# Seven half products for three pairs of projection tiles, and rotary rows turned in groups

## The chip, the cores and the metric

The kernel runs on one core of a Trainium2 chip. The metric is the device time of one execution in microseconds, as the median of the runs shown; lower is better. Engines are named as in the profile: PE does the matmuls (PEld its weight loads), DVE the element-wise work on two operands, ACT copies and activations, POOL small moves and accumulating transfers, SP issues the other transfers.

## What is computed

One encoder layer for 512 tokens of 1024 features in float32: two attention mixers side by side, merged by gates, then a SwiGLU channel mixer. Cut to what matters here:

```python
proj = h @ w_in[l]
qa, ka, va, qb, kb, vb = jnp.split(proj, SPLITS, axis=-1)
qa = rope_partial(qa.reshape(b, s, A_Q_HEADS, HEAD_DIM), pos)      # 16 heads of 64
qb = rope_partial(...)  # and kb: 12 heads each, three groups of window and dilation
o_a = windowed_gqa_sink(qa, ka, va, a_sink[l])
o_b = dilated_mixture(qb, kb, vb)
gates = jax.nn.sigmoid(h @ w_gate[l] + b_gate[l])
g_a, g_b = jnp.split(gates, N_BRANCH, axis=-1)
mixed = g_a * (o_a @ w_br_a[l]) + g_b * (o_b @ w_br_b[l])
h = layer_norm(DN_ALPHA * h + mixed @ w_out[l], ln1_g[l], ln1_b[l])
f = (jax.nn.silu(h @ w_ff_gate[l]) * (h @ w_ff_up[l])) @ w_ff_down[l]
h = layer_norm(DN_ALPHA * h + f, ln2_g[l], ln2_b[l])
```
`rope_partial` turns only the first 16 of each head's 64 features by the token's position: 8 rows against 8 rows.

## The kernel before

**Products.** The projections are computed with features on the partitions and the 512 tokens on the columns. One weight unit is 1024 x 128: it gives one tile of 128 features (two heads) by 512 tokens. Each operand is split into a rounded upper part and a rest, and a product is three matmuls (upper x upper, upper x rest, rest x upper; lines 496 to 498 in `feat_k`). Over eight slices of 128 input features a unit is 24 matmuls of 512 columns. A unit's weights come in two halves (`half_unit`): SP loads a 128 x 512 half, ACT or DVE copies the upper part (`split`), DVE subtracts (line 383). The input is split in the same way at the start, into eight pairs that stay (lines 464 to 469).

**The channel mixer already uses seven half products.** Its two units of one index form a 2 x 2 block product over halves of the 1024 features and of the tokens (the `Quad` class): sums of weight blocks (S1 to S4) and of token blocks (T1 to T4) are formed and split, and seven products of 12 matmuls with 256 columns each take the place of eight (lines 1422 to 1424).

**Rotation.** A projected tile of queries or keys is turned by `rotate`: four DVE rows over all 128 partitions (lines 517 to 523), though only 16 of every 64 rows change. It is then split, and `q_post` and `k_post` move the parts to where the scores need them, by transfers from SP.

**Order.** Two things set it. `ORDER` is a list of steps written by hand: `VA` are the values of the first mixer, `q1` to `q7` and `k1` its query and key tiles (`q0`, `k0` come first of all), `A0` to `A3` its head groups of four heads and four blocks of queries each, `g` a gate tile, `Q00 K00` and so on the second mixer's query and key tiles, `V12 V0` its values, `B0` to `B3` its heads. Each step hands operations with their costs to a planner (`Program`). The planner goes through time with its own cost table and lets each engine take the first ready operation by priority, within limits on buffers: 85 slots of 128 x 512 in all, of them 6 for weights as loaded (`ws`), 12 for split weights (`whl`), the rest for general use, and eight PSUM banks, three of them for projections (`dense`). What it chose is the order in which each engine's instructions stand in the program; on the chip each engine works them off in that order and waits for what is not there yet.

**A head group** needs scores from PE, their minimum with mask and sink on DVE (line 798), the exponential on ACT (802), a reciprocal and a scaling (805, 739), transposes on PE (749), a split on ACT and DVE (754), the products with values on PE (815, 816), and a last sum on DVE (828). The values' own split is at 695.

**The end of the stage.** When the eight heads and groups are done, all slots go to the rest of the layer (`free_all`): branch products, gates times branches, output product, norm, channel mixer, norm.

Of the kernel before, what the change touches and what calls it, by code (L numbers as in the profile page):

```python
# [15 lines left out]
P = 128  # L16
# [44 lines left out]
UNITS = 2  # L61
SPIN = 4
# [6 lines left out]
N_WS, N_WHL, N_ATT = 6, 12, 16  # L69
# [10 lines left out]
g2 VA q1 A0 q2 q3 A1 g k1 q4 g q5 A2 g q6 g q7 A3 g2  # L80
Q00 K00 Q01 K01 V12 Q02 K02 V0 B0 Q10 K10 B1 Q11 K11 Q12 K12 B2 B3 g8
"""

# [34 lines left out]
class Program:  # L118
# [67 lines left out]
    def run(self):  # L186
# [26 lines left out]
        while n_left:  # L213
# [11 lines left out]
            while progress:  # L225
                progress = False
                for e in engines:
# [14 lines left out]
                    cost = dict(o.alts)[e]  # L242
# [12 lines left out]
                    if e == SP:  # L255
                        end = now + 0.47
                        moved = max(moved, now + 0.9) + (1.5 if now < 5 else 0.92) * cost
                        o.done = moved + 0.87
                    elif o.moves:
                        end = now + cost  # L260
                        moved = max(moved, end + 0.3) + 0.92 * o.moves
                        o.done = moved + (0.87 if e == ACT else 2.2)
                    else:
                        end = now + cost
                        o.done = end
# [50 lines left out]
def hybrid_layer(ctx: ExitStack, tc: tile.TileContext, wpack, xT, xtok, sink, bgate,  # L316
# [9 lines left out]
                  "ws": N_WS, "whl": N_WHL, "att": N_ATT, "gen": N_SLOT - 2 - N_ATT - N_WS - N_WHL,  # L326
# [34 lines left out]
    def f32(ap):  # L361
        return ap.bitcast(F32)

    def load(b, src, cost=0.73, prio=0.0, abs_prio=None, dst=None, after=()):
        return op([(SP, cost)], lambda e: nc.sync.dma_start(dst() if dst else b.t, src), writes=[b],
                  prio=prio, abs_prio=abs_prio, after=after)
# [21 lines left out]
    def half_unit(u, j):  # L388
        st, h, l = slot(F32, "ws"), slot(F32R, "whl"), slot(F32R, "whl")
        load(st, wpack[u, :, j * S:(j + 1) * S], prio=-LOOK)  # L390
        split(st, h, l, prio=-LOOK, hold=[(l, "room")])
        return h, l

# [61 lines left out]
    got = {}  # L455
    for j in range(KD):
        st, ap = slot(F32, "xs"), FIRST["x"][j]

# [51 lines left out]
    EV, NORM = -100.0, -150.0  # L510


    SHUF = list(range(8, 16)) + list(range(0, 8)) + list(range(16, 32))

    def rotate(ps):
        R, Sh = slot(), slot()
# [135 lines left out]
    def turned_values(u, nt, turn_by=0, done=None):  # L652
# [3 lines left out]
        for i in range(2):  # L656
# [16 lines left out]
            op(cp_alts(S, True, 0.3 if turn_by else 0.1)[:2 if turn_by else 1], evac, reads=[ps], writes=[t], prio=EV)  # L673
# [327 lines left out]

    def gate(f, put=False):
# [36 lines left out]
    env = {"gate": 0, "qs": {}, "ks": {}}  # L1039

    def step(w):
        if w == "VA":
# [15 lines left out]
        elif w[0] in "QK":  # L1058
            pair, g = int(w[1]), int(w[2])
            u = U_QKB + 6 * pair + 2 * g + (w[0] == "K")  # L1060
            if w[0] == "Q":
                env["qs"][pair, g] = dense_q(u, 4 if g == 0 else 0, (0, 1))
            else:
                env["ks"][pair, g] = dense_k(u, 8 if g == 0 else 0)
# [198 lines left out]
    def copy_by_act(dst, src, n, ps, reads, writes, prio=NORM):  # L1263
        op([(ACT, act(n, ps))], lambda e: copy(ACT, dst(), src()), reads=reads, writes=writes, prio=prio)

# [41 lines left out]
    LO, HI = slice(0, HP), slice(HP, S)  # L1307
    su, uf = {}, {}
    silus = []

    def tt(dst, x, y, o, reads, writes, w=HP, prio=EV):
        op([(DVE, dve(w))], lambda e: nc.vector.tensor_tensor(dst(), x(), y(), op=o), reads=reads, writes=writes,  # L1312
           prio=prio)

    def parts(h, l, src, reads, n, prio, whole=True):

        copy_by_act(h[0], src, n, False, reads, [h[1], l[2]], prio)
        tt(l[0], src, lambda: f32(h[0]()), ALU.subtract, [*reads, h[1]], [l[1]], n, prio)

    def hl(st, prio):  # L1320
        h, l = slot(F32R, "whl"), slot(F32R, "whl")
        parts((lambda: h.t, h), (lambda: l.t, l, (l, "room")), lambda: st.t, [st], S, prio)
        return h, l


# [451 lines left out]
```

## Time and profile before

| | us |
|---|---|
| median of 3 runs | 737.72 (737.66 to 737.75) |
| the profiled execution | 737.0 |
| its span, from the first to the last instruction | 735.2 |
| PE busy / DVE busy / ACT busy | 725.2 / 653.7 / 447.4 |

The span's times in windows and rows are microseconds from its start. A row in a timeline reads: start, busy time, engine, line, operation, what it writes and reads, partitions of the weights, shape and type, count; behind it in brackets the idle time before it and what ended that. Busy times of rows that follow each other overlap, so the distance of two starts is what a row costs on a full engine. A row in the list of waits reads: who waited, for whom, us in total, how often, the longest. The granted clock was 0.999 over the span.

### The profile page before, as it was taken

Reading aid. Unit: us, or ns where it says so; the run is one execution under the profiler, and the core shown is the slowest. Engines: PE = TensorE matmul, PEld = TensorE weight load, DVE = VectorE, ACT = ScalarE, POOL = GpSimd, SP = SyncE. Lnnn points to the kernel's source line nnn. Section 1 sums busy time; section 2 is a strip of 40 time slices with the busy share of each in tenths; the row PEclk is TensorE's granted clock in tenths of the full one; section 3 lists DMA queues with packets and bytes.
Section 4 is the critical chain, followed back from the end, with each engine's and each line's share of the span. In section 5 each row is a group of like instructions: output and inputs, shape, how many; then the busy total and the mean of one; then the engine's idle time right before and its main releaser. Section 6 shows DMA issues by size and latency. Waiting matters only on the chain.

```text
span 735.2 us, 13431 instructions
## 1 busy us (share of the span) xinstructions
PE 725.2 (99%) x4479; PEld 663.0 (90%) x4479; DVE 653.7 (89%) x1428; ACT 447.4 (61%) x1012; POOL 109.5 (15%) x273
## 2 busy tenths in 40 slices
PE   9999999999999999999999999999999999999995
PEld 6888888888888889888888999999999999999985
DVE  5879998898898999897686999799999999899977
ACT  5647687757665657774352567656666556666721
POOL 0000110000003323500010002111102111202100
PEclk9999999999999999999999999999999999999999
DMA  8824523437234765455583389776888978978402
GB/s 270 289 58 144 163 82 87 129 94 204 76 93 138 201 176 163 137 170 174 165 205 88 86 250 233 178 179 154 203 254 195 221 196 237 243 196 180 112 29 86
DMA packets 69252, 120.17 MB, mean 163 GB/s; under 512 B 8576, under 2 KB 12800, under 8 KB 69184
## 3 DMA queue, kind: packets, MB, share of 16 engines
q1 hardware_dynamic: 59040, 101.10, 44.7%
q0 software_dynamic: 9872, 18.09, 15.2%
q8 instruction: 35, 0.57, 0.3%
q14 instruction: 33, 0.27, 0.1%
q10 hardware_dynamic: 272, 0.13, 0.1%
HBM read 103.04 MB, written 2.10 MB: 143 GB/s over the span
## 4 chain that ended last, share of the span: by engine, by line
PE 94%; DMA 2%; DVE 2%; SPq 1%; ACT 1%; issue 0%; DVEq 0%; ACTq 0%
PE ps L497 12%; PE ps L496 12%; PE ps L498 12%; PE ps L1422 9%; PE ps L1424 9%; PE ps L1423 9%; PE ps L1633 4%; PE ps L1635 4%; PE ps L1634 4%; PE ps L749 3%; PE ps L1192 3%; PE ps L1193 3%; PE ps L1194 3%; PE ps L647 1%; PE ps L646 1%; PE ps L815 1%
## 5 line engine op out<-in xcount | busy, mean ns | idle before, releaser
L357 ACT ACTIVATE sl<-sl 128x512 fp32r<-128x512 f32 (+3 forms) x383 | 210.6, 582 | 62.0 <-DVE sl L1312 17.3
L1312 DVE TENSOR_TENSOR sl<-sl,sl 128x512 fp32r<-128x512 f32 (+3 forms) x294 | 167.1, 609 | 6.2 <-ACT sl L357 3.4
L357 ACT ACTIVATE sl<-ps 128x256 f32<-128x256 f32 (+5 forms) x205 | 85.8, 441 | 99.7 <-PE ps L1424 60.1
L496 PE MATMUL ps<-x,sl 128*128 128x512 f32 (+1 forms) x369 | 142.4, 386 | 0.3 <-ACT x L357 0.3
L498 PE MATMUL ps<-x,sl 128*128 128x512 f32 (+1 forms) x369 | 139.8, 379 | 0.0
L497 PE MATMUL ps<-x,sl 128*128 128x512 f32 (+1 forms) x337 | 127.9, 379 | 0.2 <-DVE x L469 0.2
L1422 PE MATMUL ps<-sl,sl 128*128 128x256 f32 x352 | 96.9, 275 | 0.6 <-ACT sl L357 0.6
L1423 PE MATMUL ps<-sl,sl 128*128 128x256 f32 x352 | 96.8, 275 | 0.0
L1424 PE MATMUL ps<-sl,sl 128*128 128x256 f32 x352 | 96.8, 275 | 0.0
L383 DVE TENSOR_TENSOR sl<-sl,sl 128x512 fp32r<-128x512 f32 x130 | 87.2, 685 | 5.1 <-ACT sl L357 4.5
L498 PEld LDWEIGHTS ps<-x,sl 128*128 128x128 f32 x369 | 69.9, 189 | 9.9 <-DVE sl L406 0.2
L496 PEld LDWEIGHTS ps<-x,sl 128*128 128x128 f32 x369 | 70.2, 190 | 8.7 <-ACT x L357 0.5
L371 POOL DMA_DIRECT2D sl<-wpack x44 | 38.5, 883 | 260.3 <-DMA sl<-wpack 72.7
L1422 PE MATMUL ps<-x,sl 128*128 128x256 f32 x264 | 72.6, 275 | 0.0
L1423 PE MATMUL ps<-x,sl 128*128 128x256 f32 x264 | 72.6, 275 | 0.0
L1424 PE MATMUL ps<-x,sl 128*128 128x256 f32 x264 | 72.6, 275 | 0.0
L497 PEld LDWEIGHTS ps<-x,sl 128*128 128x128 f32 x337 | 64.0, 190 | 7.5 <-DVE x L469 0.5
L1422 PEld LDWEIGHTS ps<-sl,sl 128*128 128x128 f32 x352 | 67.6, 192 | 0.8 <-ACT sl L357 0.7
L1423 PEld LDWEIGHTS ps<-sl,sl 128*128 128x128 f32 x352 | 67.6, 192 | 0.1
L1424 PEld LDWEIGHTS ps<-sl,sl 128*128 128x128 f32 x352 | 67.6, 192 | 0.0
L1422 PEld LDWEIGHTS ps<-x,sl 128*128 128x128 f32 x264 | 50.6, 192 | 0.4
L1423 PEld LDWEIGHTS ps<-x,sl 128*128 128x128 f32 x264 | 50.6, 192 | 0.4
(151 smaller groups left out, 1547.1 us busy)
## 6 DMA issues: line engine op xcount, KB each, us to landing
sl<-wpack SPq DMA_DIRECT2D x243, 256.0 KB, 3.7
sl<-sl SPq DMA_DIRECT2D x108, 128.0 KB, 2.3
wf<-wpack SPq DMA_DIRECT2D x51, 256.0 KB, 5.0
sl<-wpack POOLq DMA_DIRECT2D x44, 256.0 KB, 5.9
wf<-wpack POOLq DMA_DIRECT2D x24, 256.0 KB, 6.3
sl<-xtok SPq DMA_DIRECT2D x8, 256.0 KB, 3.3
out<-sl SPq DMA_DIRECT2D x7, 256.0 KB, 2.0
sl<-xT SPq DMA_DIRECT2D x6, 256.0 KB, 5.6
```

Of the source, the lines that this page charges most:

```text
L357: nc.scalar.activation(dst, src, AF.Copy)
L371: op([(POOL, 1.0)], lambda e: nc.gpsimd.dma_start(b.t, src2, accum_op=ALU.add), reads=[b], writes=[b], prio=prio, moves=1.65)
L383: op([(DVE, dve(S))], lambda e: nc.vector.tensor_tensor(l.t, src.t, f32(h.t), op=ALU.subtract), reads=[src, h], writes=[l], prio=prio, abs ...
L496: mm(o, a, x0, start=(k == 0 and begins), stop=False, skip_group_check=split)
L497: mm(o, a, x1, start=False, stop=False, skip_group_check=split)
L498: mm(o, b, x0, start=False, stop=(k == nk - 1), skip_group_check=split)
L1312: op([(DVE, dve(w))], lambda e: nc.vector.tensor_tensor(dst(), x(), y(), op=o), reads=reads, writes=writes, prio=prio)
L1422: mm(o, wh, pairs(bh[k]()), start=(first and k == 0), stop=False, skip_group_check=True)
L1423: mm(o, wh, pairs(bl[k]()), start=False, stop=False, skip_group_check=True)
L1424: mm(o, wl, pairs(bh[k]()), start=False, stop=(k == 3), skip_group_check=True)
L1633: mm(ps.t, x0, pairs(w[0].t), start=(first and m == 0), stop=False, skip_group_check=True)
L1634: mm(ps.t, x0, pairs(w[1].t), start=False, stop=False, skip_group_check=True)
```

## The change

Three pairs of tiles are computed by seven half products as in the channel mixer: `q5` with a gate, `q6` with `q7`, and two gates. For them the input's tiles are kept after they were split, and token sums T1 to T4 are formed from them in place and split once (`x_forms`, step `X`); the eight split pairs stay in 16 general slots until the last pair. The new tiles, and all second-mixer query and key tiles, go to SBUF unturned; their rotary rows are gathered by SP into one tile (two or three tiles' rows, 64 or 96 partitions), turned there by four DVE rows, and sent back (`turn_rows`, step `R`). Gates of pairs are sent to DRAM and fetched again when needed. Until the last pair is done the limits are 8, 16 and 60 slots (`L` sets the first two back). The planner's costs change for the first 300 us, so its order moves there in many places. The diff, cut:

```diff
-g2 VA q1 A0 q2 q3 A1 g k1 q4 g q5 A2 g q6 g q7 A3 g2
-Q00 K00 Q01 K01 V12 Q02 K02 V0 B0 Q10 K10 B1 Q11 K11 Q12 K12 B2 B3 g8
+g2 VA q1 A0 q2 q3 g X k1 q4 A1 P:q5,g P:q6,q7 R A2 P:g,g A3 g g2 L Q00 K00 R Q01 K01 R V12 Q02 K02 R V0 B0 Q10 K10 R Q11 K11 R B1 Q12 K12 R B2 B3 g7
...
-                    cost = dict(o.alts)[e]
+                    cost = dict(o.alts)[e] * (1.03 if e == DVE and now < 110 else 1.0)
...
-                        end = now + 0.47
-                        moved = max(moved, now + 0.9) + (1.5 if now < 5 else 0.92) * cost
-                        o.done = moved + 0.87
+                        end = now + (0.62 if 14 < now < SLOW else 0.47)
+                        moved = max(moved, now + 0.9) + (1.5 if now < 9.5 else 1.0 if now < SLOW else 0.92) * cost
+                        o.done = moved + (2.4 if 14 < now < SLOW else 0.87)
...
+    def x_forms():
+        at = lambda k, n: (lambda b=xs[k]: b.t[:, n * HP:(n + 1) * HP])
...
+        for k in range(KD // 2):
...
+            tt(x11, x11, x12, ALU.subtract, a, a, HP, FORMS)
+            tt(x12, x22, x12, ALU.subtract, a + b, a, HP, FORMS)
+            minus_sum(x22, x11, x22)
+            minus_sum(x21, x22, x21)
+            for kk, toks in ((k, a), (k + 4, b)):
+                h, l = slot(F32R), slot(F32R)
+                parts((lambda h=h: h.t, h), (lambda l=l: l.t, l, (l, "room")), lambda b=xs[kk]: b.t, toks, S, FORMS)
...
+    def pair_x(ua, ub):
...
+        for key in ("A11", "S1", "A12", "S3", "A22"):
+            fetch(key)
+        sep("A11")
+        sep("A12")
+        form("S2", "A11", "S1", "A11")
+        sep("S2")
+        sep("S1")
+        form("S4", "A12", "A12", "S2")
+        for key in ("S3", "S4", "A22"):
+            sep(key)
+        y, xz, t, v = bank("dense"), bank("dense"), slot(), slot()
...
+        product("A11", "B11", y, "y", LO, True)
+        keep(t, LO, 1, y, "y", LO)
+        product("A12", "B21", xz, "x", LO, True)
+        product("S2", "T2", y, "y", LO, False)
+        keep(t, HI, 2, y, "y", LO)
+        product("S1", "T1", xz, "z", HI, True)
+        keep(v, HI, 2, xz, "z", HI)
+        product("S3", "T3", y, "y", LO, False)
+        product("S4", "B22", xz, "z", HI, False)
...
+        tt(both, both, lambda: xz.t.rearrange("p (c b a) -> p c a b", c=2, a=2), ALU.add,
+           [(t, 1), (t, 2), (xz, "x"), (xz, "z")], [(t, 1), (t, 2)], S)
+        op([(DVE, dve(HP))], lambda e: nc.vector.scalar_tensor_tensor(
+            halves(v.t[:, HI]), back(y.t[:, LO]), -1.0, halves(v.t[:, HI]), op0=ALU.mult, op1=ALU.subtract),
+           reads=[(v, 2), (y, "y")], writes=[(v, 2)], prio=EV)
+        product("A22", "T4", y, "y", LO, False)
+        keep(v, LO, 1, y, "y", LO, -1.0)
...
+    def turn_rows(tiles):
...
+        for i, R in enumerate(tiles):
+            for h in range(2):
...
+                op([(SP, 0.1)], lambda e, R=R, i=i, h=h: nc.sync.dma_start(
+                    G.t[32 * i + 16 * h:32 * i + 16 * h + 16], R.t[64 * h:64 * h + 16]), reads=[(R, 1), (R, 2)], writes=[gs[-1]], prio=EV)
...
+        op([(DVE, dve(S, extra=0.03))], lambda e: nc.vector.stream_shuffle(h_(), g(), SHUF2), reads=gs, writes=[H], prio=EV)
+        op([(DVE, dve(S))], lambda e: nc.vector.tensor_tensor(g(), g(), c.t[0:n], op=ALU.mult),
...
+        op([(DVE, dve(S))], lambda e: nc.vector.tensor_tensor(g(), g(), h_(), op=ALU.add), reads=[*gs, H], writes=gs, prio=EV)
```

The first place is DVE's start, while the input tiles (`x`) arrive. Before, DVE has the rests of the input (line 469) and of the first weights (406) alone:

```order
L469 TENSOR_TENSOR x411_103<-sl1_71,x47_94 128x512
L406 TENSOR_TENSOR sl16_118<-sl6_85,sl15_117 128x128
L406 TENSOR_TENSOR sl10_101<-sl3_75,sl9_100 128x128
L406 TENSOR_TENSOR sl13_109<-sl5_83,sl12_108 128x128
L406 TENSOR_TENSOR sl16_118<-sl6_85,sl15_117 128x128
L469 TENSOR_TENSOR x411_103<-sl8_98,x47_94 128x512
L406 TENSOR_TENSOR sl10_101<-sl3_75,sl9_100 128x256
```
In the changed order, from the same row on (486 was 469, 422 was 406; 534 is the sum helper, here with token sums in place):

```order
L486 TENSOR_TENSOR x411_103<-sl1_71,x47_94 128x512
L534 TENSOR_TENSOR sl2_73<-sl2_73 128x256
L534 TENSOR_TENSOR sl1_71<-sl1_71 128x256
L486 TENSOR_TENSOR x411_103<-sl8_98,x47_94 128x512
L422 TENSOR_TENSOR sl10_101<-sl3_75,sl9_100 128x256
L422 TENSOR_TENSOR sl13_110<-sl5_83,sl12_109 128x256
L422 TENSOR_TENSOR sl16_118<-sl6_85,sl15_117 128x256
L534 TENSOR_TENSOR sl8_98<-sl8_98 128x256
L486 TENSOR_TENSOR x411_103<-sl17_130,x47_94 128x512
L534 TENSOR_TENSOR sl17_130<-sl17_130 128x256
```
The token sums stand between the input's rests, each behind the rest of the tile that it overwrites.

The second place is PE in the second pair (`q6`, `q7`), of which the changed order has these rows (629 to 631 are the three matmuls of a half product, 860 and 861 scores of a head group; `ps268` is the pair's first bank, `ps272` its second). Before, no such rows stand there: these tiles are units of 24 matmuls with 512 columns at lines 496 to 498.

```order
L629 MATMUL ps268_1142<-sl116_523,sl260_1095 128x256
L630 MATMUL ps268_1142<-sl117_524,sl260_1095 128x256
L631 MATMUL ps268_1142<-sl116_523,sl261_1096 128x256
L860 MATMUL ps298_1293<-sl95_428,sl161_676 128x384
L861 MATMUL ps298_1293<-sl96_429,sl161_676 128x384
L860 MATMUL ps299_1298<-sl95_428,sl162_683 128x384
L861 MATMUL ps299_1298<-sl96_429,sl162_683 128x384
L629 MATMUL ps272_1163<-x432_211,sl265_1135 128x256
L630 MATMUL ps272_1163<-x434_219,sl265_1135 128x256
L631 MATMUL ps272_1163<-x432_211,sl266_1136 128x256
```
The first three rows end S3 T3, the last three begin S4 B22; nine more rows of it and eight transposes follow, and then A22 T4 writes the first bank again. No projection of another tile stands between.

The third place is SP where the rotary rows of `q5`, `q6` and `q7` are gathered (702) and sent back (713), in the changed order; 371 are weight loads, 1225 a gate sent away. Before, SP has only loads and the moves of split parts there.

```order
L702 DMA sl284_1229<-sl276_1182 16x512 x2
L371 DMA sl315_1379<-wpack 128x512
L702 DMA sl284_1229<-sl297_1289 16x512 x2
L371 DMA sl321_1402<-wpack 128x512
L371 DMA sl325_1422<-wpack 128x512
L371 DMA sl332_1458<-wpack 128x512
L371 DMA sl337_1485<-wpack 128x512
L371 DMA sl345_1529<-wpack 128x512
L713 DMA sl250_1045<-sl284_1229 16x512 x2
L713 DMA sl276_1182<-sl284_1229 16x512 x2
L713 DMA sl297_1289<-sl284_1229 16x512 x2
L1225 DMA gz359_1595<-sl319_1394 128x512
```
Weight loads stand between and behind the gathers, five of them between the last gather and the first row sent back.

214 lines of the change are left out of this document (188 added, 26 removed).

## The prediction, as put on record

> **What bounds the kernel now.** I read the page's busy line and its chain of waits first, then what the matrix engine (PE) waited for, then a table by stage, and last the vector engine's (DVE's) own waits in the first stage.
>
> ```profile
> PE 725.2 (99%) x4479; PEld 663.0 (90%) x4479; DVE 653.7 (89%) x1428; ACT 447.4 (61%) x1012; POOL 109.5 (15%) x273
> ...
> PE 94%; DMA 2%; DVE 2%; SPq 1%; ACT 1%; issue 0%; DVEq 0%; ACTq 0%
> ```
> ```profile
> PE ps L433 <- DVE eps L483: 1.2, 1, 1.2
> PE ps L1422 <- ACT sl L357: 0.6, 1, 0.6
> PE ps L1192 <- DVE sl L1126: 0.4, 1, 0.4
> PE ps L496 <- ACT x L357: 0.3, 1, 0.3
> PE ps L497 <- DVE x L469: 0.2, 1, 0.2
> ```
> The second block is all that PE waited for in 735.2 us: 2.7 us, of which 1.7 us lie before 13 us. PE is the bound nearly everywhere, so PE work that is taken out comes out of the time, unless another engine then holds PE up. Which one could is in the table by stage (columns: window, its length, busy us and count of PE, PEld, DVE, ACT, POOL):
>
> ```profile
> 0.00:6.00 6.00, 4.80 (x15) 2.47 (x15) 1.87 (x7) 2.72 (x6) 0.90 (x5) 1.00 0.56 159
> 6.00:60.00 54.00, 53.51 (x257) 46.34 (x257) 43.35 (x95) 31.20 (x66) 4.01 (x15) 1.00 0.64 211
> 60.00:130.00 70.00, 70.00 (x383) 62.64 (x382) 63.85 (x162) 54.21 (x127) 6.70 (x25) 1.00 0.39 112
> 130.00:240.00 110.00, 110.00 (x590) 98.18 (x589) 100.75 (x271) 71.73 (x182) 12.06 (x54) 1.00 0.44 123
> 240.00:340.00 100.00, 100.00 (x546) 89.49 (x545) 93.70 (x245) 67.99 (x169) 26.88 (x107) 1.00 0.60 175
> ```
> From 60 to 340 us DVE is busy 258.3 of 280 us, 92%. It is the second bound, and the change lays work on it. ACT (193.9 of 280) has room.
>
> **What the change takes from PE.** A unit is 24 matmuls of 512 columns, a pair of units 48. The seven half products of a pair are 84 matmuls of 256 columns. The spacing of each kind, from starts:
>
> ```profile
> 345.33 0.38 PE L496 MATMUL ps<-x,sl 128*128 128x512 f32 x1
> ...
> 349.87 0.38 PE L496 MATMUL ps<-sl,sl 128*128 128x512 f32 x1
> ```
> ```profile
> 419.77 0.28 PE L1423 MATMUL ps<-x,sl 128*128 128x256 f32 x1
> ...
> 422.57 0.28 PE L1424 MATMUL ps<-x,sl 128*128 128x256 f32 x1
> ```
> The first block is 22 rows in a run: 4.54 us / 21 = 0.2162 us. The second is 26 rows: 2.80 / 25 = 0.1120 us. A pair so goes from 48 x 0.2162 = 10.38 to 84 x 0.1120 = 9.41 us: 0.97 us less, **2.91 us for three pairs**. The busy column (0.38 and 0.28) must not be used here, since the rows overlap. The order confirms the count: 144 matmuls of 512 columns fewer, 252 of 256 more, and nothing else changes on PE.
>
> The Trainium skill, page "TensorE: Matmul & The Clock Gate", section "Back-to-back issue gap", says that the spacing is set by the weight load and the matmul together, about 81 ns at 128 columns and 131 ns at 512. An estimate from that page, on a line between its two figures, is 98 ns at 256, and a pair would then go from 6.3 to 8.2 us, 5.8 us more for three; the rows above disagree with it on both sizes, and they decide.
>
> **What it puts on DVE, and where.** Two rows of equal kind start 0.60 us apart at 512 columns and 0.33 us at 256:
>
> ```profile
> 59.97 0.68 DVE L523 TENSOR_TENSOR sl<-sl,sl 128x512 f32<-128x512 f32 x1
> 60.57 0.68 DVE L383 TENSOR_TENSOR sl<-sl,sl 128x512 fp32r<-128x512 f32 x1
> ...
> 423.51 0.42 DVE L1312 TENSOR_TENSOR sl<-sl,ps 128x256 f32<-128x256 f32 x1
> 423.84 0.69 DVE L1312 TENSOR_TENSOR sl<-sl,sl 128x512 f32<-128x512 f32 x1
> ```
> A turn is four such rows (the shuffle has 0.63), 2.43 us. By the order 15 of 22 turns go (-36.5 us) and 7 grouped ones come. A grouped turn works on 64 or 96 partitions, and that price is in the trace too:
>
> ```profile
> 28.22 0.69 DVE L565 TENSOR_TENSOR sl<-sl,sl 64x512 fp32r<-64x512 f32 x1
> 28.82 0.69 DVE L521 TENSOR_TENSOR sl<-sl,sl 128x512 f32<-128x512 f32 x1
> ```
> 64 partitions take what 128 take (0.60 from start to start), so 7 x 2.43 = +17.0 us. Splits and sums of weights and token forms: 35 more, 12 fewer, 23 x 0.60 = +13.8. Sixteen 256-wide token sums, x 0.33 = +5.3. The pairs' own sums, 3 x (0.60 + 0.33) = +2.8. Copies and scalings that the planner moved from ACT to DVE, about a dozen of 0.26 to 0.60: +5. Sum: **about +7 us on DVE**, in a stage where it has 22 us free and PE becomes 2.9 us shorter. Over the whole stage it fits.
>
> It does not lie evenly. The token forms and the first weights stand early, the saved turns late. I counted the rows ahead of one marker in both orders: the first transpose of head group A0 that needs a scaled probability. On PE 18 matmuls of 512 columns and a transpose more stand ahead of it, 18 x 0.2162 + 0.11 = 4.0 us. On DVE 30 rows more: 16 of 512 columns (9.6 us) and 16 of 256 (5.3), less some copies (0.8): 14.1 us. So DVE must find 10.1 us of free time before the marker. Before, PE reached it here, and DVE had let these waits pass:
>
> ```profile
> 61.05 0.71 PE L749 MATMUL ps<-ident,sl 128*128 128x128 f32 x5
> ```
> ```profile
> DVE sl L695 <- ACT sl L357: 4.4, 2, 4.1
> DVE x L469 <- ACT x L357: 1.8, 2, 1.0
> DVE sl L383 <- ACT sl L357: 1.3, 2, 0.8
> DVE sl L517 <- PE ps L498: 0.9, 1, 0.9
> DVE sl L406 <- ACT sl L357: 0.9, 2, 0.6
> DVE nsink L479 <- DMA nsink<-sink: 0.7, 1, 0.7
> DVE bg L481 <- DMA bg<-bgate: 0.2, 1, 0.2
> ```
> DVE's free time from 6 to 60 us is 54 - 43.35 = 10.65 us, nearly all of it in these waits (the waits before 6 us are for the first data, and no form can fill them). The change needs 10.1 of the 10.65. Most of it is there to be had: the x waits (1.8) have form rows put into them, and a DVE that comes later no longer finds the value split (4.4), the projection (0.9), nsink and bg (0.9) unfinished. Waits for ACT's upper halves (1.3 + 0.9) I expect to stay by more than half, since a split cannot go ahead of its copy. With some 1.5 us of waits left and 0.55 us to spare, PE waits **about 1.0 us** near 65 us, once. Bounds from these rows: 0 (all waits filled), and 10.1 us (none is filled; the whole extra work stands in PE's way). I take 1.0, near the lower end, because 8.0 of the 10.65 us are waits of the kinds that go.
>
> Behind the marker the margins are no worse. By the same count, from the marker to A0's last product with values PE has 48.6 us of rows and DVE 44.8 (before 31.6 and 29.2), to A1's last 35.2 and 31.9 (before 40.3 and 37.6), to A2's 46.5 and 42.9 (before 48.5 and 46.5). DVE has 3.3 to 3.8 us free in each piece where it had 2.0 to 2.7 and PE never waited.
>
> **What hides the rest.** ACT has 32 rows more, none dearer than a copy of 512 columns:
>
> ```profile
> L357 ACT ACTIVATE sl<-sl 128x512 fp32r<-128x512 f32 x307 | 183.3, 623 | 49.6 <-DVE sl L1312 16.4 <-DVE sl L523 9.8 <-PE ps L497 9.7
> ```
> That is 20 us at most, into 86 us that it has free from 60 to 340. SP issues some 75 transfers more, 60 of them for the turns, each of which goes out and back over its queue:
>
> ```profile
> sl<-sl SPq DMA_DIRECT2D x108, 128.0 KB, 2.3
> ```
> Two such trips and four DVE rows are about 2 x 2.3 + 2.4 = 7 us and some issues until a turned tile is there, where before only the DVE rows stood. While it runs, PE has products, gates or units of other heads; the cover ends only if a head group is the sole work left, and then one late group would cost up to 7 us. In SP's rows the gathers of the first turn stand between weight loads, so a gather that waits for its tile holds back the loads behind it; these loads are for PE rows many microseconds on. The three gates sent out and fetched again are 0.75 MB beside 120.17 MB. I cost all of this at nothing.
>
> **Sum.** Against the profiled execution (737.0 us, span 735.2, so 1.8 us lie around the span): -2.9 + 1.0 = -1.9, 735.1 us. The median of the runs is 737.72, 0.7 above that execution, so the forecast for a median is **735.8 us**.
>
> **The rivals.** All are on the median, and a measurement of this kernel can tell about 0.2% (1.5 us) from no change.
>
> - *DVE late in the first stage* (no measurable change). Of the 10.65 us of waits some 3.5 stay instead of 1.5, PE loses 3 us: 737.72 - 2.9 + 3 = 737.8 us. For it: only 0.55 us to spare. Against: the largest wait, 4.4 us, was DVE being early, not late. From 1.4 us lost it is no longer a measurable gain; up to 4.4 us it is no measurable loss.
> - *The hand-over of the product bank* (slower). A pair holds two of the three dense banks. Its fourth product into the first bank, S3 T3, must be read by DVE (the scalar-tensor-tensor of the pair) before A22 T4 may write there, and between the two PE has only S4 B22 (12 x 0.112 = 1.34 us) and some rows of an A unit, with no other projection ahead in its order. Before, the same place in the channel mixer is emptied by ACT. If DVE comes there d late, PE waits d, three times. It decides from 3 d = 2.9 + 1.5, d = 1.5 us, two or three DVE rows. With five rows, 3.0 us, it is 9.0 - 2.9 = +6.1: 743.8 us. For it: DVE at 91% and more. Against: the transposes and scores put between bring the cover to some 2.8 us.
> - *Halves do not pace at 0.112 us here.* If the weight loads were not overlapped, each would take the busy time of a load:
>
> ```profile
> L1422 PEld LDWEIGHTS ps<-x,sl 128*128 128x128 f32 x264 | 50.6, 192 | 0.4
> ```
> 84 x 0.19 = 16.0 us for a pair, 5.6 more, 754.4 us for three. Against: the same 792 products with the same loads pace at 0.112 us in the channel mixer. This is the skill's rule above as a mechanism.
> - *The change does not do what it says*: excluded by the order's counts, but for a tile that PE waits for because its turn is late; 2 in 100.
>
> **How the numbers follow.** Forecast (0 to 1.4 us lost, 734.8 to 736.2) 0.56; DVE late in the first stage (736.2 to 739.2) 0.25; bank hand-over 0.15; halves slow 0.02; the rest 0.02, shared out. Faster by over 0.2%: 0.56. Within 0.2%: 0.27. Slower: 0.17. The range is from the full 2.9 us and a little more, 734.6, to 739.6, the end of the second case and the beginning of the third; that leaves under 2 in 10 out.
>
> **What would show it.** PE's busy rows: 252 more of 256 columns at 0.112 us. PE's list of waits: a new entry of about 1 us on a DVE or ACT row between 60 and 70 us, and nothing of size after. DVE's wait of 4.4 us on the value split gone, its busy time from 6 to 60 us near 52. If PE's waits in the pairs (75 to 115 us) name the scalar-tensor-tensor or the sum over the second bank, the bank rival is right. If the list holds more than 2.9 us in all beyond today's 2.7, the gain is gone; if SP or a transfer is named for it, my costing of the turns was wrong.

## The result and the profile after

The changed kernel takes **741.04 us** (median of 6 runs, 739.78 to 741.92); the kernel before took 737.69 in the same session (6 runs). The ratio is 1.0044, interval 1.0034 to 1.0055: some 3.3 us slower, where 1.9 us faster was forecast. The profiled execution is the fastest of the six, 739.78 us with a span of 737.9: 2.7 us more than the span of before.

The first block is the page's busy line and its chain, the second all that PE waited for, the third the table by stage (columns as before: window, length, PE, PEld, DVE, ACT, POOL, clock, DMA share, GB/s).

```profile
PE 723.1 (98%) x4587; PEld 662.9 (90%) x4587; DVE 661.0 (90%) x1445; ACT 460.7 (62%) x1041; POOL 118.8 (16%) x279
...
PE 90%; DMA 5%; DVE 2%; SPq 1%; ACT 1%; issue 1%; DVEq 0%; ACTq 0%
```
```profile
PE ps L513 <- DVE sl L1387: 2.5, 1, 2.5
PE ps L449 <- DVE eps L500: 1.2, 1, 1.2
PE ps L895 <- ACT sl L363: 1.0, 1, 1.0
PE ps L513 <- ACT x L363: 0.8, 1, 0.8
PE ps L514 <- DVE x L486: 0.8, 2, 0.5
PE ps L1663 <- ACT sl L363: 0.6, 1, 0.6
PE ps L515 <- DVE sl L422: 0.4, 1, 0.4
```
```profile
6.00:60.00 54.00, 51.69 (x240) 43.13 (x241) 50.88 (x109) 34.67 (x72) 4.32 (x11) 1.00 0.80 235
60.00:130.00 70.00, 70.00 (x485) 65.83 (x484) 65.93 (x156) 53.34 (x123) 8.59 (x27) 1.00 0.66 178
130.00:240.00 110.00, 110.00 (x597) 98.10 (x596) 95.88 (x257) 76.31 (x189) 7.72 (x34) 1.00 0.40 111
240.00:340.00 100.00, 100.00 (x548) 89.54 (x547) 84.79 (x242) 65.92 (x172) 38.21 (x134) 1.00 0.57 162
340.00:400.00 60.00, 57.45 (x278) 50.14 (x277) 50.16 (x89) 30.12 (x54) 6.06 (x7) 1.00 0.72 208
```
PE's waits grew from 2.7 to 7.3 us. From 60 to 340 us, where the pairs, the grouped turns and all head groups lie, PE does not stand still once, and DVE has become freer (246.6 us busy instead of 258.3). The loss lies at the two ends: before 60 us and between 340 and 400. For the latter this is the kernel before:

```profile
340.00:400.00 60.00, 59.57 (x278) 51.83 (x277) 40.44 (x66) 21.83 (x37) 6.05 (x7) 1.00 0.59 159
```
To place the loss, I took each PE row's start less the sum of the spacings of all rows ahead of it in PE's order (0.216 us at 512 columns, 0.163 at 384, 0.112 at 256, 0.11 at 128). This is the time that PE has lost so far. The stages are cut where this sum reaches 50, 340 and 400 us, which is later in the span by what was lost until then. The first column holds the time until the first rows, which varied from 5.4 to 6.1 us between profiles; the second includes it.

| profile of | first rows | until 50 us | 50 to 340 | 340 to 400 |
|---|---|---|---|---|
| before | 5.4 | 6.6 | 0.2 | 0.7 |
| changed | 5.8 | 9.9 | 0.4 | 2.9 |
| e1 sums behind gates | 5.7 | 9.5 | 0.4 | 3.9 |
| e2 forms after slice 3 | 6.1 | 9.0 | 0.4 | 4.5 |
| e3 gates kept | 5.6 | 10.0 | 0.9 | 5.5 |
| e4 no pairs | 5.7 | 6.8 | 1.5 | 6.8 |
| e5 e1 + early fetch | 5.5 | 8.9 | 0.4 | 0.1 |
| e6 e5 + forms after input | 5.9 | 6.6 | 1.8 | 0.1 |
| e7 old costs | 5.6 | 9.0 | 13.7 | 0.6 |
| e8 before, new costs | 5.4 | 7.0 | 0.8 | 0.9 |
| e10 no pairs, split first | 5.4 | 6.8 | 0.6 | 1.2 |
| e11 single turns | 5.9 | 6.9 | 19.9 | 11.0 |
| e12 e6 + sum first | 5.5 | 7.5 | 3.1 | 0.1 |

Before to changed: 3.3 us up to 50 us, 0.2 up to 340, 2.2 after, 5.6 in all (the terms are rounded); less the 2.9 us of PE work, that is the 2.7 us of the spans. A single profile places the early loss only roughly: the changed kernel, e1 and e5 have the same rows in the same order up to 320 us, and there 9.9, 9.5 and 8.9 us until 50. What the rows show at the three places:

**12 to 20 us.** DVE's timeline, and PE's rows that stood still:

```profile
17.32 0.42 DVE L560 SCALAR_TENSOR_TENSOR sl<-sl 128x256 f32<-128x256 f32 x1
17.65 0.42 DVE L534 TENSOR_TENSOR sl<-sl,sl 128x256 f32<-128x256 f32 x1
17.99 0.68 DVE L486 TENSOR_TENSOR x<-sl,x 128x512 fp32r<-128x512 f32 x1
```
```profile
13.19 0.48 PE L514 MATMUL ps<-x,sl 128*128 128x512 f32 x1 [0.24 <-DVE x L486]
16.85 0.48 PE L515 MATMUL ps<-x,sl 128*128 128x512 f32 x1 [0.38 <-DVE sl L422]
18.73 0.48 PE L514 MATMUL ps<-x,sl 128*128 128x512 f32 x1 [0.53 <-DVE x L486]
```
Token sums (534, 560) stand ahead of the rest of an input tile (486); two of them are 0.67 us, and PE waits 0.53 us for that rest.

**43 us.** ACT's timeline, and PE's row:

```profile
41.42 1.15 ACT L363 ACTIVATE sl<-sl 128x512 fp32r<-128x512 f32 x2 [1.61 <-DVE sl L534]
42.48 0.64 ACT L363 ACTIVATE sl<-ps 128x256 f32<-128x256 f32 x2
```
```profile
43.17 0.55 PE L895 MATMUL ps<-ident,sl 128*128 128x128 f32 x3 [0.97 <-ACT sl L363]
```
ACT's two copies of token sums stand ahead of the evacuation of the values. The sums are late on DVE, ACT sits idle for 1.61 us with the evacuation behind it, and PE's transposes wait.

**380 us.** DVE's timeline, PE's row, and POOL's accumulating loads (377), two in one row:

```profile
373.89 0.69 DVE L1387 SCALAR_TENSOR_TENSOR sl<-sl,ps 128x512 f32<-128x512 f32 x1 [0.26 <-PE ps L515]
378.34 0.69 DVE L534 TENSOR_TENSOR sl<-sl,sl 128x512 f32<-128x512 f32 x1 [3.76 <-DMA sl<-wpack]
378.95 0.69 DVE L1409 TENSOR_TENSOR sl<-sl,sl 128x512 f32<-128x512 f32 x1
379.55 0.68 DVE L1387 SCALAR_TENSOR_TENSOR sl<-sl,ps 128x512 f32<-128x512 f32 x1
```
```profile
380.29 0.48 PE L513 MATMUL ps<-sl,sl 128*128 128x512 f32 x1 [2.55 <-DVE sl L1387]
```
```profile
369.95 1.78 POOL L377 DMA_DIRECT2D sl<-wpack  x2 [42.28 <-PE ps L514]
```
In the branch stage a sum of two weight blocks of the channel mixer (S2, line 534) is at the head of DVE's order. One of its blocks is completed by an accumulating transfer, the one that POOL issued at 369.95: in the trace it landed at 378.25, 8.3 us later, and the sum starts behind it. Two rows behind the sum stands the gated product (1387) that empties the bank PE needs for its next branch product. The kernel before has the sum ahead of a gated product there too (1312 is the sum, 1126 the product):

```profile
375.10 0.69 DVE L1312 TENSOR_TENSOR sl<-sl,sl 128x512 f32<-128x512 f32 x1 [2.30 <-DMA sl<-wpack]
...
376.91 0.68 DVE L1126 SCALAR_TENSOR_TENSOR sl<-sl,ps 128x512 f32<-128x512 f32 x1
```
There POOL had issued the transfer at 366.95 and it landed at 375.08, after 8.1 us, and PE stood 0.4 us. So the transfer itself was hardly slower in the changed kernel; it was issued 3.0 us later.

### The profile page after: what moved, and what is told of

Its sections match the earlier page's. It is cut to its first block, busy times and chain, and to the rows that moved or that the text cites. A ratio compares the mean times of both kernels' runs of the same rounds, so it can differ in the third digit from the quotient of the medians.

```text
span 737.9 us, 13854 instructions
## 1 busy us (share of the span) xinstructions
PE 723.1 (98%) x4587; PEld 662.9 (90%) x4587; DVE 661.0 (90%) x1445; ACT 460.7 (62%) x1041; POOL 118.8 (16%) x279
## 4 chain that ended last, share of the span: by engine, by line
PE 90%; DMA 5%; DVE 2%; SPq 1%; ACT 1%; issue 1%; DVEq 0%; ACTq 0%
PE ps L513 9%; PE ps L514 9%; PE ps L515 9%; PE ps L1663 9%; PE ps L1665 9%; PE ps L1664 9%; PE ps L1874 4%; PE ps L1876 4%; PE ps L1875 4%; PE ps L963 3%; PE ps L1453 3%; PE ps L1455 3%; PE ps L1454 3%; DMA sl<-wpack 2%; PE ps L861 1%; PE ps L860 1%
## 5 line engine op out<-in xcount | busy, mean ns | idle before, releaser
L363 ACT ACTIVATE sl<-sl 128x512 fp32r<-128x512 f32 (+3 forms) x401 | 220.9, 585 | 40.5 <-DVE sl L534 19.5
L534 DVE TENSOR_TENSOR sl<-sl,sl 128x512 fp32r<-128x512 f32 (+3 forms) x333 | 192.2, 615 | 8.0 <-DMA sl<-wpack 3.8
L363 ACT ACTIVATE sl<-ps 128x256 f32<-128x256 f32 (+6 forms) x210 | 89.9, 446 | 96.9 <-PE ps L1665 59.7
L513 PE MATMUL ps<-x,sl 128*128 128x512 f32 (+1 forms) x321 | 123.3, 384 | 0.9 <-ACT x L363 0.8
L515 PE MATMUL ps<-x,sl 128*128 128x512 f32 (+1 forms) x321 | 121.6, 379 | 0.4 <-DVE sl L422 0.4
L514 PE MATMUL ps<-x,sl 128*128 128x512 f32 (+1 forms) x289 | 109.8, 380 | 0.9 <-DVE x L486 0.8
L377 POOL DMA_DIRECT2D sl<-wpack x50 | 44.1, 886 | 314.0 <-DVE sl L534 95.2
L389 DVE TENSOR_TENSOR sl<-sl,sl 128x512 fp32r<-128x512 f32 x118 | 79.1, 684 | 3.5 <-ACT sl L363 3.1
L515 PEld LDWEIGHTS ps<-x,sl 128*128 128x128 f32 x321 | 60.7, 189 | 9.4 <-DVE sl L422 0.9
L513 PEld LDWEIGHTS ps<-x,sl 128*128 128x128 f32 x321 | 60.8, 189 | 8.8 <-ACT x L363 1.5
L514 PEld LDWEIGHTS ps<-x,sl 128*128 128x128 f32 x289 | 54.7, 189 | 8.2 <-DVE x L486 2.3
L1016 ACT ACTIVATE sl<-sl,st 128x257 f32<-128x257 f32 (+1 forms) x64 | 35.7, 560 | 26.9 <-DVE st L1012 25.0
L1663 PEld LDWEIGHTS ps<-x,sl 128*128 128x128 f32 x264 | 50.6, 192 | 0.4
```

What stands on the lines that cost most here:

```text
L363: nc.scalar.activation(dst, src, AF.Copy)
L377: op([(POOL, 1.0)], lambda e: nc.gpsimd.dma_start(b.t, src2, accum_op=ALU.add), reads=[b], writes=[b], prio=prio, moves=1.65)
L389: op([(DVE, dve(S))], lambda e: nc.vector.tensor_tensor(l.t, src.t, f32(h.t), op=ALU.subtract), reads=[src, h], writes=[l], prio=prio, abs ...
L513: mm(o, a, x0, start=(k == 0 and begins), stop=False, skip_group_check=split)
L514: mm(o, a, x1, start=False, stop=False, skip_group_check=split)
L515: mm(o, b, x0, start=False, stop=(k == nk - 1), skip_group_check=split)
```

## The experiments

Theory A: the losses come from rows at the head of DVE's and ACT's orders that wait, or are not needed yet, while rows behind them hold up PE. Rivals: B (transfers of the branch stage are late for everything), C (too much DVE work early, wherever it stands), D (the turns cost something), P (the planner's new costs), and K on the clock. Each run was timed beside the kernel before, whose medians lay from 737.37 to 737.47. To compare with the changed kernel across sessions, use the ratios.

**e1.** The sums may stand only behind the last gated product:

```diff
-                tt(lambda: dst.t, lambda: x.t, lambda: y.t, ALU.add, [x, y], [dst], S, -LOOK)
+                tt(lambda: dst.t, lambda: x.t, lambda: y.t, ALU.add, [x, y], [dst], S, -LOOK, marks[-1:])
```


> The changed kernel, but the weight sums S2 of the channel mixer's first products may stand in DVE's order only behind the last product of a gate and a branch. Only DVE's order changes (four rows of it move); PE, ACT, POOL and SP have the same rows in the same order. Theory A (a row that stands ahead in DVE's order and waits for a late accumulating transfer holds the bank's reader behind it): PE's wait of 2.5 us near 380 us goes, 741.0 - 2.2 = 738.8 us. Theory B (the transfers of that stage are late for everything, because the gates are fetched again there): another row waits in its place, 741.0 us.

Measured 738.39 us (737.16 to 740.68), ratio 1.0019 (1.0010 to 1.0028). A's number, but not A's picture: the execution that was profiled, one of its two slowest (740.29), still has PE waiting 1.9 us there, now for this DVE row:

```profile
378.53 0.69 DVE L1387 SCALAR_TENSOR_TENSOR sl<-sl,ps 128x512 f32<-128x512 f32 x1 [2.23 <-DMA sl<-gz]
```
The third of the gates sent to DRAM is late too: it took 9.1 us from issue to landing here, 7.7 in the profile of the changed kernel. So A and B are both right in part: the order puts late data at the head, and there are two late transfers.

**e2.** Token sums from the fourth input slice on (the first sum of each tile waits for that PE row):

```diff
-            tt(x11, x11, x12, ALU.subtract, a, a, HP, FORMS)
+            tt(x11, x11, x12, ALU.subtract, a, a, HP, FORMS, [hold_x])
```


> The changed kernel, but the token sums may begin only when PE has begun the fourth of eight input slices (about 14 us). PE's order and POOL's stay, DVE has some 15 rows moved, ACT three. Theory A (token sums that stand between the rests of the input and of the first weights make PE late): of the 2.1 us lost before 20 us some 1.5 go, the 1.2 us at 43 us stay, 739.5 us. Rival C (the sheer amount of DVE work ahead of the first head group makes PE late, wherever it stands): the same time is lost further on, between 20 and 70 us, 741.0 us.

Measured 740.68 us, ratio 1.0045 (1.0032 to 1.0057), no gain. Up to 50 us it lost 2.9 us from its first rows on instead of 4.1, so a part came back as A says; near 380 us it lost 4.5 instead of 2.9, since there the clock fell behind the wait (below). On its own it settles nothing.

**e3.** No gate sent out: `AWAY = ()`.

> The changed kernel, but the three gates of the pairs stay in SBUF: no transfer sends them out or fetches them again (0.75 MB fewer). The planner's order changes in many rows; in it all sums S2 stand behind the gated products. Theory A: the wait near 380 us goes because of the order, the early losses stay, 738.8 us. Theory B (gates fetched again): the same time, and then e1 tells which of the two it was.

Measured 743.57 us, ratio 1.0087. A miss for both theories: the order changed, and another row made PE wait 3.5 us, the split of the second mixer's output, with five weight splits ahead of it on DVE:

```profile
355.10 3.09 DVE L389 TENSOR_TENSOR sl<-sl,sl 128x512 fp32r<-128x512 f32 x5
358.11 0.69 DVE L1361 TENSOR_TENSOR sl<-sl,sl 128x512 fp32r<-128x512 f32 x1
```
**e4.** No pairs, no token sums; `T:` puts a whole unit into SBUF for a grouped turn:

```diff
-g2 VA q1 A0 q2 q3 g X k1 q4 A1 P:q5,g P:q6,q7 R A2 P:g,g A3 g g2 L Q00 ...
+g2 VA q1 A0 q2 q3 g k1 q4 A1 T:q5 g T:q6 T:q7 R A2 g g A3 g g2 Q00 ...
```


> The changed kernel without its three pairs: q5, q6, q7 and the three gates are whole units of 24 matmuls of 512 columns again, no token sums, the old limits on weight slots; the grouped turns, the order of steps and the planner's new costs stay. Theory A (the losses come from the token sums at the start and the order near 380 us, the turns cost nothing): the early 3.3 us and the 2.9 us of PE gain both go, the late wait may go or stay with the order, 737.7 to 739.9 us. Rival D (grouped turns make PE wait): 740 us or more with PE waiting in the head groups for a turned tile.

Measured 743.05 us, ratio 1.0080. The early loss is gone (6.8 us against 9.9 in the table), which ties it to the pairs with their token sums (e6 moves the sums alone). But the wait of e3 is there as well: 3.5 us, and 6.8 lost in that stage.

**e5.** As e1, and the gates fetched at once:

```diff
-                fetch_gate(k, [*exps, marks[names.index("b%d" % (k - 11))]] if k > 10 else exps)
+                fetch_gate(k, exps)
```


> As e1, and the three gates are fetched again as soon as the last head's exponentials are done, not one after another behind earlier gated products (in SP's order they stand 13 to 34 rows further ahead). Theory A with B (near 380 us DVE's head row waits for a late transfer, in the changed kernel the accumulated sum, in e1 the gate, and PE behind it; in profiles of e1, e2 and e4 the granted clock then falls to 0.5 to 0.7 for some 3.5 us): no PE wait there and no fall of the clock, 741.0 - 2.9 - 1.3 = 736.8 us. Rival: the earlier fetches hold back other transfers and the wait comes back elsewhere in that stage, 738.4 us as e1 or more.

Measured 736.66 us (735.89 to 737.36), ratio 0.9991 (0.9982 to 1.0000). PE waits for nothing between 20 and 680 us but the values at 43:

```profile
PE ps L449 <- DVE eps L500: 1.2, 1, 1.2
PE ps L895 <- ACT sl L363: 1.0, 1, 1.0
PE ps L1663 <- ACT sl L363: 0.6, 1, 0.6
PE ps L514 <- DVE x L486: 0.5, 1, 0.5
PE ps L515 <- DVE sl L422: 0.4, 1, 0.4
```
From 1.0044 to 0.9991 is 3.9 us, and 2.8 of them are in the branch stage of the table. That the rest is the clock's fall in most executions of the changed kernel (see e13 to e15), which its profiled one does not have, is likely but not shown: the table also has 1.0 us less before 50 us, where the order is the same. Without e1's edit e5 is the same program, row for row: once the gates are fetched early, the planner puts the sums behind the gated products by itself. So the early fetch alone brings this time, and e1's profile says that the first edit alone is not enough.

**e6.** As e5, and the token sums only from the last input slice on (e2's edit with another slice).

> As e5, and the token sums begin only when PE has begun the last of the eight input slices (about 20 us). PE's order changes in places. Theory A (position): the 3.3 us lost up to 43 us go but for some tenths, 733.8 us. Rival C (sheer amount of DVE work before the first head group and the pairs): they come back between 40 and 80 us, 736.8 us.

Measured **735.73 us** (735.25 to 736.42), ratio 0.9978 (0.9969 to 0.9987): faster than both kernels (than the one before by 0.2%). Up to 50 us the loss is that of before. But 1.4 us of the 2.3 that the table shows as saved come back later, most of it here:

```profile
115.21 0.68 DVE L390 TENSOR_TENSOR sl<-sl,sl 128x512 fp32r<-128x512 f32 x1
115.81 0.68 DVE L535 TENSOR_TENSOR sl<-sl,ps 128x512 f32<-128x512 f32 x1
116.41 0.41 DVE L653 SCALAR_TENSOR_TENSOR sl<-ps,sl 128x256 f32<-128x256 f32 x1
```
```profile
116.88 0.38 PE L630 MATMUL ps<-sl,sl 128*128 128x256 f32 x1 [1.12 <-DVE sl L653]
```
This is the bank hand-over of the prediction, once in three pairs. So in size rival C holds for over half of the sum, A for the rest; the place, near 117 us, is not the 40 to 80 us that C had named.

**e7 and e8.** The whole change with the planner's old costs, and the kernel before with the new ones (the cost lines of the diff, one way and the other).

> The whole change but with the planner's old costs: pairs, token sums, grouped turns, limits as in the changed kernel, the order as the old costs make it. Theory P (it is the new costs, which end at 300 us, that bring the stalls of the stage near 360 to 380 us): no stall there, 737 us, with an early loss of 3 us or more. Rival (the stalls come with any new order in which sums, gates and splits are packed on DVE): 740 us or more.

> The kernel before with the planner's new costs and nothing else of the change: PE has the same work as before. Theory P: a PE wait of 2 to 3.5 us near 360 to 380 us and a fall of the clock behind it, 740 to 743 us. Rival: 737.4 us, no wait over 1 us.

e7: 749.32 us, ratio 1.0158 (1.0145 to 1.0172). e8: 738.13 us, ratio 1.0009 (1.0001 to 1.0018), no PE wait over 1.2 us. With the old costs the branch stage loses 0.6 us only, as P says, but the time is not P's 737 us: the second mixer loses 13.7 us. And by e8 the new costs alone bring no stall, against P. What is shown is that the change needs the new costs. The first of the 13.7 us stands behind a gather of rotary rows, which the old costs took for quicker (0.87 us after the move for 2.4):

```profile
DVE sl L705 <- DMA sl<-sl: 4.5, 1, 4.5
```
```profile
181.33 0.79 PE L1030 MATMUL ps<-sl,sl 128*128 128x512 f32 x1 [3.80 <-DVE sl L968]
```
**e9.** As e3 with 14 matmuls on zeros ahead of the row that waits.

> As e3, and ahead of the branch product at which PE stood for 3.5 us there, PE does 14 matmuls of 512 columns on zeros into a free bank (28 instructions, 14 x 0.216 = 3.0 us if they pace as the others); they are no part of the result. DVE's row that PE waits for is not moved. Theory K (PE's standing still lets the granted clock fall, which costs 2 us behind the wait): the clock stays at 1.00 behind it, 743.6 - 2.0 = 741.6 us, though PE has more work. Rival (the fall of the clock has another cause, or is drawn by the work behind): 743.6 us or more.

Measured 745.37 us. It did not do what was meant: these matmuls put the next gated product off, DVE waited 2.31 us for it, and the split that PE needs came later by as much. PE's wait was still 2.9 us. It decides nothing on K. The profiled execution is the fastest of the four (743.42 us), and in it the clock stayed at 1.00 behind the 2.9 us.

**e10.** As e4, with the second mixer's split first (priority -160 for -20) and e1's edit.

> As e4 (no pairs, grouped turns, new costs), and the split of the second mixer's output has priority over the weight splits, so that in DVE's order it stands ahead of some five of them, and the sums S2 behind the gated products. Theory A: e4's wait of 3.5 us near 357 us and the fall of the clock behind it go, and what is left is PE's work of before with turns that cost nothing, 743.1 - 5.5 = 737.6 us. Rival D (the turns cost something in themselves): 739 us or more.

Measured 737.81 us, ratio 1.0004 (0.9995 to 1.0013). Grouped turns and new costs alone neither cost nor bring anything. D is wrong, and the pairs are what makes e6 faster than this: by the profiled spans 736.1 against 733.1, 3.0 us for 2.9 of PE work, with nearly the same time lost in the table (8.6 and 8.5 us). By the medians it is 2.1, of which 0.6 is that e6 has 2.4 us around its span and e10 1.8.

**e11.** As e6, each tile turned by itself (the calls of `turn_rows` left out).

> As e6, but each tile is turned by itself, by four DVE rows over 128 partitions (22 turns instead of 7 grouped ones, no gathers): 15 x 2.43 = 36.5 us of DVE rows more less 17.0, and 60 transfers fewer. If the grouped turns are what gives DVE the room for the pairs: PE waits in the head groups for DVE, 738 us or more. Rival (the turns give nothing, PE does not see them): 735.7 us.

Measured 763.99 us, ratio 1.0362 (1.0348 to 1.0377). The longest of PE's waits:

```profile
PE ps L630 <- ACT sl L638: 4.0, 1, 4.0
PE ps L514 <- ACT sl L364: 3.7, 1, 3.7
PE ps L515 <- DVE sl L1362: 3.3, 1, 3.3
PE ps L964 <- DVE sl L954: 3.2, 1, 3.2
```
DVE is busy 679.5 us instead of e6's 658.1, and 21 us more there became 28 us more in time. The grouped turns do not show as a gain by themselves (e10), but up to 340 us they are the room in which the pairs' sums lie: 18 us more are lost there than in e6. Some 11 us more are lost in the branch stage, where no tile is turned: twelve weight splits stand there on DVE ahead of the split that PE waits for, as in e3 and e4. Whether the turns pushed them there is not shown.

**e12.** As e6, with the pair's scalar-tensor-tensor first (`prio=EV - 200`).

> As e6, but the scalar-tensor-tensor of a pair, which empties the first bank, goes ahead of the weight splits that wait in DVE's order (seven rows in the third pair). In e6 PE waited 1.1 us for it there, and with the clock's fall behind it lost 1.4 us. Theory: this wait goes, 735.7 - 1.4 = 734.3 us. Rival (DVE is short of time there, so the splits that now stand behind make PE wait instead): 735.7 us.

Measured 737.08 us, ratio 0.9994 (0.9985 to 1.0003): the rival, and worse than it. The wait at 117 us is gone, and PE waits 0.9 us and 1.5 us for a scaling and a split between 150 and 250 us instead (another 0.9 us is lost before 50 us). With C this agrees: who is served first only moves the wait.

**e13 to e15: what a wait costs.** Behind the wait near 380 us the clock had fallen in e1's profile, and had not in that of the changed kernel (windows of 2 us; the clock is third from the end):

```profile
380.00:382.00 2.00, 2.00 (x7) 1.53 (x7) 1.84 (x4) 1.67 (x3) 0.86 (x1) 0.55 0.35 49
382.00:384.00 2.00, 2.00 (x7) 1.63 (x6) 2.00 (x5) 1.36 (x2) 0.00 (x0) 0.60 0.96 219
```
```profile
380.00:382.00 2.00, 1.71 (x8) 1.52 (x9) 1.90 (x4) 1.68 (x4) 0.86 (x1) 1.00 0.36 48
382.00:384.00 2.00, 2.00 (x11) 1.76 (x10) 2.00 (x5) 1.35 (x3) 0.00 (x0) 1.00 0.65 115
```
In e1 the clock gives up 2 x (0.45 + 0.40) = 1.7 us in those 4 us, and the matmuls start 0.43 us apart instead of 0.216: 1.7 us lost behind a wait of 1.9. To see whether waiting alone does it, the kernel before got a wait in the channel mixer, where no transfer is late (2, 4 or 6 rows in the loop):

```diff
+        if f == STAND:
+            def rows(e):
+                nc.vector.tensor_copy(padb.t[:, 0:4], y.t[:, 0:4])
+                for _ in range(4):
+                    nc.vector.tensor_tensor(pad.t, pad.t, pad.t, op=ALU.add)
+                nc.vector.tensor_copy(padb.t[:, 0:4], pad.t[:, 0:4])
+            op([(DVE, 0.0)], rows, reads=[(y, "y")], writes=[pad, padb], prio=EV - 300)
+            op([(PE, 0.0)], lambda e: mm(y.t[:, HP:HP + 64], padb.t, padb.t[:, 0:64], start=True, stop=True, skip_group_check=True),
+               reads=[padb], writes=[(y, "pad")], prio=EV - 300)
```
The small matmul writes into the bank in which a product of that unit is being summed, so, other than the expectation says, this unit's tile is not the reference's.

> The kernel before, and in one product of the channel mixer DVE does 2 more rows of 512 columns (0.60 us each) on a tile of zeros, for which one small matmul of 64 columns into an unused half of a bank makes PE wait; neither is part of the result. PE stands still about 1 to 1.5 us, once. Theory K (standing still itself lets the clock fall): too short, no fall, 737.4 + 1.3 = 738.7 us. Rival (the fall comes from the stage of late transfers): the same here.

> As e13 with 4 rows: PE stands still about 2.3 to 2.8 us. Theory K: in most executions the clock falls behind it to about half for some 3.5 us, which costs 1.7 us more, 737.4 + 2.6 + 1.7 = 741.7 us in those, 740.0 in the others. Rival: no fall, 740.0 us.

> As e13 with 6 rows: PE stands still about 3.6 to 4 us. Theory K: the clock falls in nearly every execution, 737.4 + 3.8 + 1.9 = 743.1 us. Rival: no fall, 741.2 us.

Measured 738.52, 741.43 and 742.73 us (ratios 1.0016, 1.0047, 1.0076), beside 737.41. In the profiles PE stood 0.5, 2.0 and 3.5 us. Behind 0.5 the clock stayed at 1.00. e14's executions fall into two groups: two at 739.04 and 739.19 us with a mean clock of 0.998, four from 741.36 to 741.83 with 0.995 to 0.996. The profiled one is of the second group:

```profile
506.00:508.00 2.00, 0.49 (x3) 0.47 (x4) 1.93 (x5) 0.50 (x1) 0.00 (x0) 1.00 0.31 55
508.00:510.00 2.00, 2.00 (x8) 1.39 (x7) 2.00 (x5) 0.00 (x0) 0.00 (x0) 0.75 0.00 0
510.00:512.00 2.00, 2.00 (x7) 1.60 (x6) 1.82 (x5) 0.00 (x0) 0.00 (x0) 0.50 0.00 0
512.00:514.00 2.00, 2.00 (x18) 2.00 (x18) 2.00 (x4) 0.38 (x1) 0.00 (x0) 0.89 0.39 124
```
The clock given up there is 2 x (0.25 + 0.50 + 0.11) = 1.7 us. In e15 the mean clock is 0.994 to 0.996 in all five. K holds: a wait of about 2 us lets the clock fall to half in some executions, one of 3.5 us in each, as far as times and mean clocks tell. In e3 and e4, with waits of 3.5 us, the table has 5.5 and 6.8 us lost.

The traces also show what tells a wait with a fall from one without. From its first rise on, 3.8 to 6.9 us behind the span's start and at another place in each profile, the granted clock is 1.00 or 0.50, nothing between. It changes only on a grid of 3.41 us: each stretch that ends within the span is a multiple of that (at half in e1 from 380.19 to 383.61 us, in e4 from 358.36 to 365.19). What differs is PE's idle time within one period of that grid, here in us:

| profile of | PE's wait | idle in the periods that it touches | at half behind it |
|---|---|---|---|
| changed | 2.5 | 1.80, 0.75 | none |
| e9 | 2.9 | 1.13, 1.74 | none |
| e14 | 2.0 | 0.09, 1.91 | 3.41 |
| e1 | 1.9 | 1.93 | 3.41 |
| e2 | 2.5 | 0.43, 2.09 | 3.41 |
| e3 | 3.5 | 1.01, 2.51 | 3.41 |
| e4 | 3.5 | 2.74, 0.78 | 6.83 |
| e15 | 3.5 | 2.11, 1.34 | 6.83 |

Up to 720 us, in all profiles, each period at full clock with 1.91 us idle or more is followed by one at half, and none with 1.80 or less, but for two in e7 and e11 with several shorter waits (1.72 and 1.58). In e4 and e15 the wait reaches into the first period at half, and a second one follows. A period at half costs 3.41 x 0.5 = 1.7 us. So whether a wait of 2 to 3 us is followed by a fall goes by where the grid cuts it, which is chance; one of 3.5 us leaves at least 1.75 us in one period, near the limit already.

## Why the prediction was wrong

**The steps that held.** PE's gain: three pairs give 2.9 us, by the count of rows and by e10 against e6 (3.0 us of span). The pitch of 0.112 us holds in the pairs. DVE's wait of 4.4 us on the value split is gone, and its busy time from 6 to 60 us, 50.9 us, is near the 52 given. Over the span DVE has 7.3 us more, where the sum said about 7. No wait in the pairs, none in the head groups, none at the marker near 65 us. The turns cost nothing, by e10; but the reason was incomplete, since with the old costs in the planner a gather costs PE a wait of 3.8 us (e7).

**"PE waits about 1.0 us near 65 us, once": mis-sized and in the wrong place.** It was 3.3 us up to 50 us in the profile (some 0.4 of it the first data), in five waits between 6 and 43 us; the same order lost 2.3 to 3.3 us in three profiles. I counted DVE's rows ahead of one marker and set them against its free time. That is a budget for the sum; it does not see that PE is served row by row on the way there. From 12 to 20 us PE needs each rest as soon as it can be had, so a token sum of 0.34 us ahead of a rest is 0.34 us for PE at once, whatever is free at 30 us. And I looked at DVE alone, where ACT's copies of the sums were what stood ahead of the values' evacuation. The range between 0 and 10.1 us had room for it; the value taken had not. e6 shows the size of the mistake: with the sums behind the input the early loss is that of before, and 1.4 us come back further on.

**"I cost all of this at nothing": false for the gates, and for a stage that I did not look at.** The prediction ends its search where the change's steps end, at 340 us. The branch stage behind it lost 2.2 us more than before. Two things the change brings meet there: the gates that are fetched again, and a new order with more work in this stage (DVE 50.2 us busy from 340 to 400, before 40.4; DMA share 0.72, before 0.59). The channel mixer's sum stood ahead of the product that empties PE's bank before too, but its transfer now came 3.2 us later; and behind it the third gate landed only at 377.51 (378.51 in e1), so that with the sum moved away (e1) the gated product waited for the gate. e5, without either wait, loses 0.1 us in this stage. The profile of before had shown the place: PE's wait of 0.4 us for line 1126 stands in the list that I quoted, and I read it as a small size and not as a row that stands behind a transfer with nothing to spare. Why the new order issues that transfer 3.0 us later stays open.

**What was not in any step: the price of a wait above its length.** The 2.5 us near 380 us let the clock fall in most executions, as far as their mean clocks tell. Of the changed kernel's six executions two have a mean clock of 0.997 to 0.998 (739.8 us), four 0.995 (740.8 to 741.9). The median lies 1.3 us above the profiled one; before, that distance was 0.7. Against the sum of 735.1 us for the profiled execution: 735.1 + 2.3 (early, above the 1.0) + 2.2 (branch stage) = 739.6, profiled 739.8.

**The rivals.** The first-stage rival had the right stage, and its 3 us the right size; alone it would have left no measurable change. The bank hand-over did not occur in the changed kernel, and did in e6 (1.1 us, once), where the token sums come later. The Trainium skill, page "TensorE: Matmul & The Clock Gate", section "HAM oscillation — how this bites in real kernels", warns of PE-idle gaps above some 3.4 us, with half the clock for a time behind them. The half agrees with e14 and e15 (0.50); the length of the gap does not: here 1.9 and 2.0 us were enough in part of the executions.

## What to carry to other kernels

When work is laid into the gaps of an engine that works in order, budget it row by row against the first consumer that is waiting, not as a sum up to a later marker, and look at each engine that carries a piece of it. When a change lets a planner reorder the program, look through the stages behind it too: a row at the head of an order that waits for a transfer is harmless only as long as nobody needs what stands behind it, and 0.4 us of PE waiting in the profile of before is a sign of how near that is. And price a wait of the matrix engine of some 2 to 3 us at its length and, by chance, 1.7 us more; the waits of 3.5 us here cost 1.7 to 3.4 us above their length.

## What the runs showed of the hardware that was not expected

- The granted clock fell to 0.50 for 3.41 us or a multiple of it, on a grid of 3.41 us whose place in the span differs between executions. A period of that grid with 1.91 us or more of idle PE was followed by one at half in every profile; behind single waits that left 1.74 and 1.80 us in one period (e9, 2.9 us long, and the changed kernel, 2.5) it was not. So a wait of 1.9 us can cost 1.7 us more and one of 2.9 us nothing.
- The same transfer of 256 KB, a gate fetched again, took 5.0, 4.3 and 7.7 us from issue to landing within 23 us of the changed kernel, the last at a DMA share of 0.86; fetched some 20 to 40 us earlier in e5, the median of the three was 2.8. The accumulating transfer beside the last one took 8.3 us, and 8.1 in the kernel before.
